# A decoder layer with dilated attention: the output matmuls of attention issued three steps behind their scores instead of two, with five buffers for the probabilities

## The chip, the cores and the metric

The kernel runs on one core of a Trainium2 chip. The time is device microseconds of one launch; the kernel before has a median of 2238.2 us over 3 runs (2236.06 to 2238.77).

## What is computed

One decoder layer over 4096 tokens of width 1024. The input is normalised per row and projected once; three groups of heads read the projection: 4 heads of a gated MLP over chunks of 128, 8 heads of causal attention in strided windows, 4 heads of attention over 256 memory tokens. Each is multiplied by a SiLU gate, concatenated, projected out and added to the input. The changed part is the strided attention:

```
for window, dil in ((128, 1), (512, 4), (2048, 16)):
    s = q . k / 8            # a block of 128 queries against its own and the previous block of keys
    s = where(0 <= rel <= window // dil, s, -inf)
    o_i, denominator_i = softmax(s) @ v
out = sum_i softmax(log denominators)_i * o_i
```

## The kernel before

**Passes.** Pass A (to about 650 us) normalises and transposes the input, and projects V and the first four heads' Q and K, which go to DRAM. Pass B projects the other four heads' Q and K and the gate of attention; pass C projects what the gated MLP and the memory heads need and computes both. The strided attention is a generator (`attn_all`), of which `merge` (line 59) takes some steps for each step of pass B and of pass C, at a higher priority. The output stage at the end (`fps`, line 937) is a run of matmuls of its own, from some 1870 us on.

**Attention of a head.** It has two stages. `attn_max` finds for each query the largest score of all three windows: 96 matmuls `pa` (line 467) go to PSUM tiles of which there are two, VectorE adds the mask and takes row maxima (`jk`, `mx`, line 474). The maxima are put into one layout by way of DRAM (`md`, line 482), of five transposes (`pm`, line 491) and of small DMAs into `cm` (lines 484 and 493), and VectorE takes their minimum with sign reversed (lines 495 and 497). `attn_main` then computes 48 steps, each of two query blocks. A step has its scores `s` by eight matmuls (lines 564 and 566; the second of a pair also subtracts the maximum, by a row of `q2` that a DMA fills from `cm`, line 512), adds the mask on VectorE (`e`, line 569), takes the exponential on ScalarE (line 571), and splits it into an F16 high half `ph` (ScalarE, line 520) and a low half `pl` (GpSimd, line 521). The output matmuls are three for each block of keys (lines 587, 589 and 591), with `ph`, `ph` and `pl` as weights; a step has up to twelve. Every four query blocks ScalarE copies the sum out (`ot`, line 596) and SyncE's queue writes it to `od`.

While the 48 steps of head h run, the maxima of head h+1 are computed between them (`mp_stage`, line 619), and near their end `q`, `k` and the rest of head h+1 are loaded (`load2`). `qn` and `kp`, which the maxima read, have one buffer; `vr`, the values, has three, of which a window uses two.

**The lag.** The output matmuls of a step are a closure that is put on a list `pend`; `drain(2)` issues all but the last two of the list, so a step's closure runs two steps after its scores, and `drain(0)` issues the rest at the end of a head. A step's closure reads its own `ph` and `pl` and those of the step before it (`prev`). `ph` and `pl` have four buffers each, which the memory heads share (line 799); `e` has four, the score PSUM tile two.

**Who sets the order.** The lines of the program give each instruction its priority; a scheduler then sets, when the kernel is built, the order on each engine by priorities and its own timeline, and places instructions that it takes to be ready. Engines run their queues in that order, one instruction after the other, and wait by semaphores.

Of the kernel before, what the change touches and what calls it, by code (L numbers as in the profile page):

```python
# [9 lines left out]
F16 = mybir.dt.float16  # L10
# [8 lines left out]
P = 128  # L19
# [52 lines left out]
def tile_hybrid_layer(ctx, tc, x, mem, norm_gain, w_in, gv_gain, wsT, gb, aqg, akg,  # L72
# [381 lines left out]
    at = at_cm.__enter__()  # L454
# [60 lines left out]
    G.memset(k2[64:65, :], 32768.0)  # L515

    def split_p(e, w, nm):
        ph = at.tile([P, 512], F16, name=f"ph{nm}", tag="ph", bufs=4)
        pl = at.tile([P, 512], F16, name=f"pl{nm}", tag="pl", bufs=4)
        S.copy(ph[:, :w], e[:, :w])  # L520
        G.tensor_sub(pl[:, :w], e[:, :w], ph[:, :w])  # L521
        return ph, pl

    def attn_main(h, q1, k1):
        pend = []

        def drain(k):
            while len(pend) > k:
                pend.pop(0)()

        for ci, d in list(enumerate(DILS))[::ORD]:
            nb = NT // d
            vts = []
            for i in range(2):
# [4 lines left out]
                else:  # L539
                    vt = at.tile([P, nb, d // 2, VW], F16, name=f"vr{h}_{ci}_{i}", tag="vr",  # L540
                                 bufs=3)
# [10 lines left out]
            for r in range(d):  # L552
                prev = None
                for b0 in range(0, nb, 2):
                    nm = f"{h}_{ci}_{r}_{b0}"
                    st = ps_tile("ps", [P, 2, 256], F32, f"s{nm}")
                    last = b0 + 2 >= nb
                    w = 384 if last else 512
                    for i in range(2):
                        b = b0 + i  # L560
                        k0 = r + b * P * d
                        n = 256 if b + 1 < nb else 128
                        kk = slice(k0, k0 + (P - 1) * d + 1, d)
                        TE.matmul(st[:, i, :n], k1[:, kk], packed(q1, d, r, b, n), start=True,  # L564
                                  stop=False)
                        TE.matmul(st[:, i, :n], k2[:, kk], packed(q2, d, r, b, n), start=False,  # L566
                                  stop=True)
                    e = at.tile([P, 512], F32, name=f"e{nm}", tag="e", bufs=4)
                    V.tensor_tensor(e[:, :w], st.rearrange("p a q -> p (a q)")[:, :w],  # L569
                                    masks[d][:, :w], ALU.add)  # L570
                    S.activation(e[:, :w], e[:, :w], AF.Exp, scale=asg[:, 2:3])  # L571
                    ph, pl = split_p(e, w, nm)

                    def pv(r=r, b0=b0, ph=ph, pl=pl, prev=prev, ci=ci, d=d, nb=nb, vblk=vblk, og=og):
                        for i in range(2):
                            b = b0 + i
                            slot = (r * nb + b) % 4
                            if slot == 0:
                                og[0] = ps_tile("po", [P, 4, 65], F32, f"o{h}_{ci}_{r}_{b}")
                            o = og[0]  # L580
                            terms = [(ph, pl, i * 256, b)]
                            if b:
                                terms.append((ph, pl, 128, b - 1) if i else
                                             (prev[0], prev[1], 384, b - 1))
                            for j, (hi, lo, c, vb) in enumerate(terms):
                                v = vblk(r, vb)
                                TE.matmul(o[:, slot, 0:65], hi[:, c:c + 128], v[:, 0:65],  # L587
                                          start=(j == 0), stop=False)
                                TE.matmul(o[:, slot, 0:64], hi[:, c:c + 128], v[:, 66:130],  # L589
                                          start=False, stop=False)  # L590
                                TE.matmul(o[:, slot, 0:65], lo[:, c:c + 128], v[:, 0:65],  # L591
                                          start=False, stop=(j == len(terms) - 1))
                            if slot == 3:
                                ot = at.tile([P, 4, 65], F32, name=f"ot{h}_{ci}_{r}_{b}", tag="ot",
                                             bufs=2)
                                S.copy(ot, o)  # L596
                                if d == 4:
                                    ov = o_d[ci].rearrange("(b m r j) h c -> r b m j h c", b=nb,
                                                           r=d, j=8)
                                    for i in range(4):  # L600
                                        Q.dma_start(ov[r, b - 3 + i, :, :, h, :], ot[:, i, :])
                                else:
                                    ov = o_d[ci].rearrange("(x p) h c -> p x h c", p=P)
                                    x1 = r * nb + b + 1
                                    Q.dma_start(ov[:, x1 - 4:x1, h, :], ot)

                    pend.append(pv)
                    drain(2)
                    prev = (ph, pl)
                    yield  # L610
        drain(0)
# [33 lines left out]
    def m_stage(h):  # L645
        cur[0] = h
        yield from attn_main(h, *mains[h])
# [119 lines left out]
    def mem_attn(n, qn):  # L767
        qd = pm.tile([P, 4, 2, HD], F16, name=f"qd{n}", tag="hl", bufs=2)
        q2t = q2ts[0]
        S.copy(qd, qn.unsqueeze(2).broadcast_to([P, 4, 2, HD]))  # L770
        V.tensor_sub(q2t[:, :, 0:64], qn, qd[:, :, 0, :])
        if n % 2 == 0:
            qms[0] = pm.tile([P, 2, 2, 4, P], F16, name=f"qm{n}", tag="stg", bufs=2)
        Q1m, Q2m = qms[0][:, n % 2, 0], qms[0][:, n % 2, 1]
        Q.dma_start_transpose(Q1m, qd.rearrange("p s a c -> p (s a c)"))
        m4 = pm.tile([P, 4], F32, name=f"m4{n}", tag="m4")
        for hp in range(2):
            pa = ps_tile("pa", [P, 2, 256], F32, f"mpa{n}_{hp}")
            for i in range(2):
                TE.matmul(pa[:, i, :], Q1m[:, 2 * hp + i, :], K1m[:, 2 * hp + i, :],  # L780
                          start=True, stop=True)
            V.tensor_reduce(m4[:, 2 * hp:2 * hp + 2], pa, AX.X, ALU.max)
        V.tensor_scalar(q2t[:, :, 64], m4, -(2.0 ** -15), msg[:, 3:4], ALU.mult, ALU.add)
        Q.dma_start_transpose(Q2m, q2t.rearrange("p s c -> p (s c)"))
        yield
        o = ps_tile("po", [P, 4, 65], F32, f"mo{n}")
        for hp in range(2):
            st = ps_tile("ps", [P, 2, 2, P], F32, f"ms{n}_{hp}")
            for i in range(2):
                h = 2 * hp + i  # L790
                for b in range(2):
                    kk = slice(b * P, (b + 1) * P)
                    TE.matmul(st[:, i, b, :], K1m[:, h, kk], Q1m[:, h, :], start=True,
                              stop=False)
                    TE.matmul(st[:, i, b, :], K2m[:, h, kk], Q2m[0:65, h, :], start=False,
                              stop=True)
            if not pools:
                e = at.tile([P, 512], F32, name=f"me{n}_{hp}", tag="e", bufs=4)
                ph = at.tile([P, 512], F16, name=f"mph{n}_{hp}", tag="ph", bufs=4)
                pl = at.tile([P, 512], F16, name=f"mpl{n}_{hp}", tag="pl", bufs=4)  # L800
            else:
                e = pools[0].tile([P, 512], F32, name=f"me{n}_{hp}", tag="fx", bufs=3)
                phl = pools[0].tile([P, 2, 512], F16, name=f"mp{n}_{hp}", tag="fx", bufs=3)
                ph, pl = phl[:, 0, :], phl[:, 1, :]
            S.activation(e, st.rearrange("p a b q -> p (a b q)"), AF.Exp, scale=msg[:, 2:3])
            S.copy(ph, e)
            G.tensor_sub(pl, e, ph)
            for i in range(2):
                h = 2 * hp + i
                for b in range(2):  # L810
                    c = (2 * i + b) * P
                    v = Vm[:, b, h, :]
                    TE.matmul(o[:, h, 0:65], ph[:, c:c + P], v[:, 0:65], start=(b == 0),
                              stop=False)
                    TE.matmul(o[:, h, 0:64], ph[:, c:c + P], v[:, 66:130], start=False,
                              stop=False)
                    TE.matmul(o[:, h, 0:65], pl[:, c:c + P], v[:, 0:65], start=False,
                              stop=(b == 1))
        rd = pm.tile([P, 4], F32, name=f"rd{n}", tag="rd")
        V.reciprocal(rd, o[:, :, 64])  # L820
        V.tensor_tensor(ym[n], o[:, :, 0:64], bcast(rd, HD), ALU.mult)
        yield
# [159 lines left out]
```

## Time and profile before

| | us |
|---|---|
| median of 3 runs | 2238.2 |
| profiled execution | 2232.59 |
| its span | 2230.9 |
| TensorE busy in it | 2018.8 |
| VectorE busy | 1568.5 |
| ScalarE busy | 1046.4 |
| GpSimd busy | 975.4 |

The profiled execution is one execution with the hardware profiler on; the span runs from its first to its last instruction. Engines are PE (TensorE), DVE (VectorE), ACT (ScalarE), POOL (GpSimd) and SP (SyncE, whose own queue is SPq and which issues the DMAs). A busy time is the union of the instructions' times; matmuls are pipelined, so a busy TensorE need not be one at its peak. Names are those of tiles in the program, with buffer numbers left out; `out<-in` says what an instruction writes and reads. `[6.87 <-DVE mx L474]` at the end of a row says that the engine was idle for 6.87 us just before it, and which instruction ended that.

### The profile page before, as it was taken

Reading aid. Unit: us, or ns where it says so; the run is one execution under the profiler, and the core shown is the slowest. Engines: PE = TensorE matmul, PEld = TensorE weight load, DVE = VectorE, ACT = ScalarE, POOL = GpSimd, SP = SyncE. Lnnn points to the kernel's source line nnn. Section 1 sums busy time; section 2 is a strip of 40 time slices with the busy share of each in tenths; the row PEclk is TensorE's granted clock in tenths of the full one; section 3 lists DMA queues with packets and bytes.
Section 4 is the critical chain, followed back from the end, with each engine's and each line's share of the span. In section 5 each row is a group of like instructions: output and inputs, shape, how many; then the busy total and the mean of one; then the engine's idle time right before and its main releaser. Section 6 shows DMA issues by size and latency. Waiting matters only on the chain. (4 is left out here: it accounts for less than half of the span.)

```text
span 2230.9 us, 44658 instructions
## 1 busy us (share of the span) xinstructions
PE 2018.8 (90%) x16481; PEld 1271.2 (57%) x16481; DVE 1568.5 (70%) x4297; ACT 1046.4 (47%) x1950; POOL 975.4 (44%) x696
## 2 busy tenths in 40 slices
PE   4888888978789899888999998998998999999998
PEld 3333333434346556455677676675775766666676
DVE  7776755477777867678688677776786667677662
ACT  5434433222236546456376465564675663222221
POOL 1455455465358657666365354453563550000000
PEclk8999998989899999999999999999999999999999
DMA  9989797775456674765545537446345347677762
GB/s 265 222 216 240 193 228 171 191 173 141 122 151 146 169 191 115 191 157 140 158 103 134 140 87 170 115 94 165 82 112 120 87 103 216 203 219 221 216 194 73
DMA packets 539675, 358.76 MB, mean 161 GB/s; under 512 B 365120, under 2 KB 474816, under 8 KB 537664
## 3 DMA queue, kind: packets, MB, share of 16 engines
q1 hardware_dynamic: 539456, 355.91, 62.8%
q8 instruction: 129, 2.11, 0.4%
q14 instruction: 90, 0.74, 0.1%
HBM read 198.52 MB, written 113.84 MB: 140 GB/s over the span
## 5 line engine op out<-in xcount | busy, mean ns | idle before, releaser
L521 POOL TENSOR_TENSOR pl<-e,ph 128x512 f16<-128x512 f32 (+1 forms) x384 | 414.8, 1095 | 305.7 <-ACT ph L520 228.9
L222 PE MATMUL pc<-wC,xTc 128*128 128x512 f16 (+1 forms) x2304 | 477.1, 351 | 6.0 <-DVE r_wO L160 5.2
L474 DVE CUSTOM_DVE_ANT_0 jk<-pa,mask 128x256 bf16<-128x256 f32 (+1 forms) x768 | 302.7, 394 | 60.9 <-PE pa L467 42.1
L222 PE MATMUL fps<-wO,fyT 128*128 128x256 f16 (+1 forms) x2304 | 341.2, 309 | 0.0
L571 ACT ACTIVATE e<-e,gas 128x512 f32<-128x512 f32 (+1 forms) x384 | 253.0, 673 | 178.7 <-DVE e L569 176.1
L222 PEld LDWEIGHTS <-xTc 128*128 128x128 f16 x2304 | 223.8, 101 | 158.6 <-issue 15.3
L222 PEld LDWEIGHTS <-xTa 128*128 128x128 f16 x1608 | 164.4, 103 | 258.4 <-issue 89.6
L569 DVE TENSOR_TENSOR e<-s,mask 128x512 f32<-128x512 f32 (+1 forms) x384 | 234.1, 626 | 69.8 <-PE s L566 50.4
L222 PEld LDWEIGHTS <-fyT 128*128 128x128 f16 x2304 | 224.5, 98 | 101.9 <-issue 1.6
L222 PEld LDWEIGHTS <-xTb 128*128 128x128 f16 x1536 | 152.0, 101 | 178.5 <-issue 28.1
L222 PE MATMUL pv<-wV,xTa 128*128 128x512 f16 (+1 forms) x840 | 194.3, 394 | 49.4 <-DVE vt L276 34.4
L520 ACT CAST ph<-e 128x512 f16<-128x512 f32 (+1 forms) x384 | 211.5, 567 | 28.8 <-PE o L591 19.0
L222 PE MATMUL pqb<-wQ,xTb 128*128 128x512 f16 x768 | 195.7, 398 | 13.1 <-DMA xTb<-xTd 8.9
L291 POOL COPY stpA<-stgA 128x1024 f16<-128x1024 f16 x32 | 153.4, 4820 | 102.0 <-DMA stgA<-hl 55.9
L291 POOL COPY stpB<-stgB 128x1024 f16<-128x1024 f16 x32 | 153.5, 4798 | 97.2 <-DMA stgB<-hl 84.1
L564 PE MATMUL s<-q,k 128*128 128x256 f16 (+1 forms) x768 | 180.3, 266 | 15.1 <-DMA q<-qkpd 5.4
L222 PE MATMUL pag<-wAG,xTb 128*128 128x512 f16 x768 | 186.3, 386 | 3.8 <-DVE sg L699 3.5
L222 PE MATMUL pq<-wQ,xTa 128*128 128x512 f16 x768 | 176.9, 388 | 12.2 <-ACT rw_q L248 8.1
L467 PE MATMUL pa<-kp,qn 128*128 128x256 f16 (+1 forms) x768 | 138.7, 270 | 52.0 <-DVE mx L474 38.0
L566 PE MATMUL s<-q,k 65*128 65x256 f16 (+1 forms) x768 | 172.1, 266 | 3.7 <-DMA q<-cm 3.7
L587 PE MATMUL o<-vr,ph 128*128 128x65 f16 x1368 | 169.5, 194 | 2.9 <-ACT ot L596 1.8
L591 PE MATMUL o<-vr,pl 128*128 128x65 f16 x1368 | 159.6, 193 | 11.1 <-POOL pl L521 11.0
(274 smaller groups left out, 3511.5 us busy)
## 6 DMA issues: line engine op xcount, KB each, us to landing
vr<-vd SPq DMA_DIRECT2D x48, 520.0 KB
fo<-od SPq DMA_DIRECT2D x96, 260.0 KB
od<-ot SPq DMA_DIRECT2D x128, 130.0 KB
x_a<-in_x_dram SPq DMA_DIRECT2D x32, 512.0 KB
xTd<-xTa SPq DMA_DIRECT2D x32, 512.0 KB
xTb<-xTd SPq DMA_DIRECT2D x32, 512.0 KB
xTc<-xTd SPq DMA_DIRECT2D x32, 512.0 KB
fx<-in_x_dram SPq DMA_DIRECT2D x32, 512.0 KB
```

Source lines behind the costliest of these rows:

```text
L222: TE.matmul(ps[:, :n], xt[:, a, k, :], w[:, b, k, c:c + n], start=(k == 0 and a == 0 and b == 0), stop=(k == KT - 1 and a == 1))
L291: G.tensor_copy(stp[:, :, half].rearrange("p s (r j) -> p s j r", r=R16), stg[:, :, half].rearrange("p s (j r) -> p s j r", r=R16))
L467: TE.matmul(pa[:, i, 256 - w:256], qn[:, q0:q0 + (P - 1) * d + 1:d], packed(kp, d, r, max(b - 1, 0), w), start=True, stop=True)
L474: V.tensor_tensor_reduce(jk[:, :w], pa[:, i, 256 - w:256], masks[d][:, 256 - w:256], 1.0, -3e38, ALU.add, ALU.max, mx[:, mc:mc + 1])
L520: S.copy(ph[:, :w], e[:, :w])
L521: G.tensor_sub(pl[:, :w], e[:, :w], ph[:, :w])
L564: TE.matmul(st[:, i, :n], k1[:, kk], packed(q1, d, r, b, n), start=True, stop=False)
L566: TE.matmul(st[:, i, :n], k2[:, kk], packed(q2, d, r, b, n), start=False, stop=True)
L569: V.tensor_tensor(e[:, :w], st.rearrange("p a q -> p (a q)")[:, :w], masks[d][:, :w], ALU.add)
L571: S.activation(e[:, :w], e[:, :w], AF.Exp, scale=asg[:, 2:3])
L587: TE.matmul(o[:, slot, 0:65], hi[:, c:c + 128], v[:, 0:65], start=(j == 0), stop=False)
L591: TE.matmul(o[:, slot, 0:65], lo[:, c:c + 128], v[:, 0:65], start=False, stop=(j == len(terms) - 1))
```

## The change

The list `pend` keeps three closures instead of two before one is issued, and `ph` and `pl` have five buffers instead of four, in `split_p` and where the memory heads take tiles of the same tag. Nothing else is edited.

```
     def split_p(e, w, nm):
-        ph = at.tile([P, 512], F16, name=f"ph{nm}", tag="ph", bufs=4)
-        pl = at.tile([P, 512], F16, name=f"pl{nm}", tag="pl", bufs=4)
+        ph = at.tile([P, 512], F16, name=f"ph{nm}", tag="ph", bufs=5)
+        pl = at.tile([P, 512], F16, name=f"pl{nm}", tag="pl", bufs=5)
...
                     pend.append(pv)
-                    drain(2)
+                    drain(3)
...
-                ph = at.tile([P, 512], F16, name=f"mph{n}_{hp}", tag="ph", bufs=4)
-                pl = at.tile([P, 512], F16, name=f"mpl{n}_{hp}", tag="pl", bufs=4)
+                ph = at.tile([P, 512], F16, name=f"mph{n}_{hp}", tag="ph", bufs=5)
+                pl = at.tile([P, 512], F16, name=f"mpl{n}_{hp}", tag="pl", bufs=5)
```

Since the scheduler sets the order, it comes out anew on all engines from the first steps of attention on. Three places follow. Heads are numbered from 0, and a name carries its head first: `jk3_0_2` is a row maximum of head 3.

VectorE's queue at the change to head 2, in the kernel before (`cm2` holds the maxima of head 2, `jk3`, `mx3` and `pa3` belong to the maxima of head 3):

```order
L269 TENSOR_TENSOR rw_q1_28_9928<-rw_q1_28_9928,gaq_591 128x256
L495 TENSOR_TENSOR cm2_9347<-cm2_9347 32x128
L497 TENSOR_TENSOR cm2_9347<-cm2_9347 32x8x16
L288 TENSOR_TENSOR hl1_28_9942<-rw_q1_28_9928,hl1_28_9942 128x8x64
L474 ISA jk3_0_0_9629,mx3_9625<-pa3_0_0_9626,mask1_739 128x128
```

The same place in the changed kernel:

```order
L474 ISA jk3_0_0_9619,mx3_9615<-pa3_0_0_9616,mask1_739 128x128
...
L474 ISA jk3_0_1_9621,mx3_9615<-pa3_0_0_9616,mask1_739 128x256
...
L474 ISA jk3_0_2_9697,mx3_9615<-pa3_0_1_9694,mask1_739 128x256
...
L474 ISA jk3_0_3_9699,mx3_9615<-pa3_0_1_9694,mask1_739 128x256
...
L495 TENSOR_TENSOR cm2_9334<-cm2_9334 32x128
```

Four row maxima of head 3, which read its first two `pa` tiles, have moved ahead of line 495.

TensorE's queue at the same place, weight loads left out, in the kernel before:

```order
L467 MATMUL pa3_0_0_9626<-kp_3_9621,qn_3_9620 128x256
...
L467 MATMUL pa3_0_1_9706<-kp_3_9621,qn_3_9620 128x256
...
L467 MATMUL pa3_0_2_9735<-kp_3_9621,qn_3_9620 128x256
...
L467 MATMUL pa3_0_3_9766<-kp_3_9621,qn_3_9620 128x256
...
L566 MATMUL s2_2_1_0_9510<-q2_3666,k2_3667 128x256
```

And in the changed kernel (the projection `pag` stands 14 times, the output matmuls between the first and the last that are shown are 24):

```order
L467 MATMUL pa3_0_1_9694<-kp_3_9611,qn_3_9610 128x256
...
L222 MATMUL pag26_10026<-wAG_3719,xTb26_9385 128x512
...
L587 MATMUL o1_0_0_28_9448<-vr1_0_1_8667,ph1_0_0_28_9313 128x65
...
L591 MATMUL o1_0_0_28_9448<-vr1_0_1_8667,pl1_0_0_30_9361 128x65
...
L467 MATMUL pa3_0_2_9725<-kp_3_9611,qn_3_9610 128x256
```

The last output matmuls of head 1 and a projection have come between the second and the third `pa` of head 3, where the `pa` stood next to each other.

VectorE's queue at the change to head 5, in the kernel before, from the fourth row maximum of head 6 on:

```order
L474 ISA jk6_0_4_17321,mx6_17220<-pa6_0_2_17318,mask1_739 128x256
...
L474 ISA jk6_0_6_17352,mx6_17220<-pa6_0_3_17349,mask1_739 128x256
...
L474 ISA jk6_0_8_17433,mx6_17220<-pa6_0_4_17430,mask1_739 128x256
...
L495 TENSOR_TENSOR cm5_16871<-cm5_16871 32x128
L474 ISA jk6_0_9_17435,mx6_17220<-pa6_0_4_17430,mask1_739 128x256
```

And in the changed kernel:

```order
L474 ISA jk6_0_2_17243,mx6_17210<-pa6_0_1_17240,mask1_739 128x256
...
L474 ISA jk6_0_3_17245,mx6_17210<-pa6_0_1_17240,mask1_739 128x256
...
L495 TENSOR_TENSOR cm5_16858<-cm5_16858 32x128
L497 TENSOR_TENSOR cm5_16858<-cm5_16858 32x8x16
L474 ISA jk6_0_4_17311,mx6_17210<-pa6_0_2_17308,mask1_739 128x256
```

Here line 495 has moved the other way: it follows four row maxima of head 6 where it followed nine.

## Rows read from the trace of the kernel before

**Rows 1.** The page: span; busy us, share of the span, instructions of two engines

```profile
span 2230.9 us, 44658 instructions
PE 2018.8 (90%) x16481; PEld 1271.2 (57%) x16481; DVE 1568.5 (70%) x4297; ACT 1046.4 (47%) x1950; POOL 975.4 (44%) x696
```

**Rows 2.** Windows by stage: busy us and count of each engine, granted clock, DMA

```profile
660.00:1825.00 1165.00, 1080.70 (x10906) 745.35 (x10905) 864.47 (x2672) 701.43 (x1395) 648.05 (x509) 0.97 0.54 131
...
1825.00:1925.00 100.00, 96.32 (x806) 66.04 (x804) 73.93 (x191) 35.62 (x45) 10.18 (x9) 0.97 0.75 211
1925.00:2231.00 306.00, 299.70 (x2325) 210.49 (x2322) 190.80 (x461) 75.17 (x74) 0.00 (x0) 1.00 0.61 185
```

**Rows 3.** Waits of PE over the span: us in total, times, longest

```profile
PE pa L467 <- DVE mx L474: 38.0, 27, 6.9
...
PE o L591 <- POOL pl L521: 11.0, 20, 1.1
...
PE pa L467 <- DMA qn<-qnd: 8.2, 4, 3.4
...
PE s L564 <- DMA q<-qkpd: 5.4, 2, 2.8
...
PE s L566 <- DMA q<-cm: 3.7, 3, 2.8
...
PE s L564 <- DMA k<-knd: 3.2, 1, 3.2
...
PE o L587 <- ACT ph L520: 1.0, 2, 0.5
```

**Rows 4.** Timeline of PE, change to head 2: start, us, instruction, idle before

```profile
939.65 0.44 PE L564 MATMUL s<-q,k 128*128 128x256 f16 x2 [2.85 <-DMA q<-qkpd]
...
951.74 0.58 PE L467 MATMUL pa<-kp,qn 128*128 128x256 f16 x2 [6.87 <-DVE mx L474]
...
952.78 0.58 PE L467 MATMUL pa<-kp,qn 128*128 128x256 f16 x2 [0.46 <-DVE mx L474]
...
953.85 0.37 PE L566 MATMUL s<-q,k 65*128 65x256 f16 x1 [0.49 <-DMA q<-cm]
```

**Rows 5.** Timeline of DVE, change to head 2

```profile
945.31 3.97 DVE L495 TENSOR_TENSOR cm<-cm 32x128 f16<-32x128 f16 x1 [6.83 <-DMA cm<-rw]
...
950.47 0.27 DVE L474 CUSTOM_DVE_ANT_0 jk<-pa,mask 128x128 bf16<-128x128 f32 x1
```

**Rows 6.** Window behind it

```profile
950.00:960.00 10.00, 7.09 (x47) 5.32 (x47) 8.66 (x35) 4.42 (x10) 2.78 (x3) 0.51 0.58 152
```

**Rows 7.** Instructions of `ph`: count, ns min/median/max, first and last start

```profile
L587 PE MATMUL o<-vr,ph x1368: 191/193/262, 656.5 to 1823.4; 128*128 128x65 f16 x196
...
L520 ACT CAST ph<-e x384: 493/602/635, 655.9 to 1815.5; 128x512 f16<-128x512 f32 x128, 128x384 f16<-128x384 f32 x64
L521 POOL TENSOR_TENSOR pl<-e,ph x384: 907/1156/1611, 656.5 to 1816.1; 128x512 f16<-128x512 f32 x128, 128x384 f16<-128x384 f32 x64
```

**Rows 8.** Timeline of PE: first and last output matmul of the last 24

```profile
1822.75 0.19 PE L587 MATMUL o<-vr,ph 128*128 128x65 f16 x1
...
1823.45 0.19 PE L591 MATMUL o<-vr,pl 128*128 128x65 f16 x1
```

**Rows 9.** Timeline of PE: 19 projection matmuls in a row

```profile
1449.84 4.26 PE L222 MATMUL pc<-wC,xTc 128*128 128x512 f16 x19
```

**Rows 10.** Timeline, change to head 5

```profile
1396.68 0.21 DVE L495 TENSOR_TENSOR cm<-cm 32x128 f16<-32x128 f16 x1 [4.46 <-DMA cm<-rw]
...
1402.15 0.31 PE L566 MATMUL s<-q,k 65*128 65x256 f16 x1 [2.79 <-DMA q<-cm]
```

**Rows 11.** Timeline, change to head 4

```profile
1249.65 0.21 DVE L495 TENSOR_TENSOR cm<-cm 32x128 f16<-32x128 f16 x1 [8.92 <-DMA cm<-rw]
1251.61 0.38 PE L467 MATMUL pa<-kp,qn 128*128 128x256 f16 x2 [0.72 <-DVE mx L474]
```

**Rows 12.** Waits of SyncE's queue

```profile
SPq L605 <- ACT ot L596: 130.8, 56, 9.0
...
SPq L543 <- PE o L591: 19.6, 9, 4.4
```

**Rows 13.** Waits of ACT

```profile
ACT ph L520 <- PE o L591: 19.0, 18, 2.9
```

**Rows 14.** Instructions of line 495: ns min/median/max

```profile
L495 DVE TENSOR_TENSOR cm<-cm x8: 204/212/3970, 644.2 to 1686.1; 32x128 f16<-32x128 f16 x8
```

**Rows 15.** Timeline of POOL, change to head 2

```profile
945.12 4.71 POOL L291 COPY stpB<-stgB 128x1024 f16<-128x1024 f16 x1 [7.82 <-DMA stgB<-hl]
```

## The prediction

> **What bounds the kernel now.** I read the page's busy shares first, then the windows by stage, the waits of TensorE, and last the timeline around the moments where the kernel passes from one attention head to the next. TensorE is the engine that bounds: it is busy 2018.8 us of a span of 2230.9, the next one, VectorE, 1568.5 [rows 1]. The windows split this. While attention runs (660 to 1825 us) TensorE is busy 1080.7 of 1165 us; in the 100 us behind it 96.3, and in the last 306 us 299.7 [rows 2]. So what is left to win in the changed stage is at most the 84.3 us that are not busy there, and whatever the tail does, it is full already: attention that ends a little sooner or later is worth its own TensorE time and nothing more.
>
> The waits of TensorE say what the idle time is made of [rows 3]. Waiting for the low halves of the probabilities (`pl`), the wait that a longer lag attacks by its nature, costs 11.0 us in 20 waits, the longest 1.1 us; the high halves (`ph`) cost 1.0 us. More is waited for the maximum of the next head (`pa` behind `mx`, 38.0 us over the whole run) and for what is loaded at a change of head: `qn` 8.2, `q` from `qkpd` 5.4, `q` from `cm` 3.7, `k` 3.2 us.
>
> The change to head 2 (heads are numbered from 0; the maxima of head 2 are done, its scores and the maxima of head 3 begin) shows how these belong together [rows 4, 5]. TensorE sits idle 2.85 us before the first score, then 6.87 us before the maximum matmuls of the next head, with 0.46 and 0.49 us behind. VectorE in that time waits 6.83 us for a DMA of `cm`, at line 495; the row maxima (L474) that free the two PSUM buffers of `pa` stand behind that instruction in its queue and start at 950.47. After it the granted clock is 0.51 of full speed over 950 to 960 us [rows 6], that is mostly the 1.2 GHz level, with 7.09 us of TensorE work in it.
>
> **The change part by part.** No arithmetic is added or removed: the same 1368 matmuls of each of the three kinds, 384 casts, 384 subtractions [rows 7]. Moved is each step's group of output matmuls, one step later, with what follows from it: the eviction `ot`, the `od` writes on SyncE's queue, the release of `ph`, `pl` and of `vr`. From 656.5 to 1823.4 us there are 384 steps, so a step lasts 3.04 us on average.
>
> *Waits for `pl` and `ph` on TensorE: 11.0 + 1.0 us [rows 3].* The ends are 0 and -12.0 us. One step more is worth 3.04 us, and the longest of these waits is 1.1, so a strict shift would take all of them. But the order of the instructions is made by a scheduler that already puts other work in between: counted in the order of before, 175 of the 384 groups of output matmuls come with three younger steps' scores already issued, 137 with two; in the order of the change 205 come with three and 81 with four. About a third of the groups move, so I take a third: -4.
>
> *The change to head 2.* The order shows that in the changed kernel four row maxima stand ahead of line 495, which free both `pa` buffers, and that TensorE has 14 matmuls of 128x512 and 24 output matmuls between the second and the third `pa`. The ends: nothing of the 7.33 us (6.87 + 0.46) and of the 2.85 + 0.49 us is saved; or all 10.67, and with it the slow clock, under which 7.09 us of work take as long as 3.5 at the other level, so 3.5 us more. The wait for `cm` itself stays, and TensorE's new cover there is less than what VectorE waits: 24 output matmuls pass in 0.73 us (first at 1822.75, last at 1823.45, one step of 0.03 behind it) [rows 8], and 14 wide ones pass in 3.1, at the 4.26 us of a row with 19 [rows 9]. I take -6 of the waits and -2 of the clock: -8.
>
> *First scores of the other heads.* Counted between the last transpose of the maxima (L491) and the first matmul of L566, the order has 585 matmuls in seven changes of head before and 837 now, because more output matmuls (24 or 36 more in five of the seven) and projections with them stand there. These cover the wait for `q` from `cm`, 3.7 us in 3 [rows 3], of which 2.79 falls at the change to head 5 [rows 10]. Ends 0 and -3.7; I take -2.
>
> *The change to head 5, on the other side.* Line 495 now stands behind four row maxima of the next head instead of nine. In the kernel before VectorE waited 4.46 us there for `cm` [rows 10] with no long wait of TensorE behind it; at the change to head 4 it waited 8.92 [rows 11]. What TensorE would wait now is not in the trace. Ends: 0, when the `pa` that have their buffers last as long as the wait, and 6.87 + 3.5 = 10.4 us, when what happened at head 2 repeats itself here. I take +4, nearer to the row of this place, which is 4.46 less a little cover.
>
> *The last steps of the last head.* Three groups are left behind the last scores instead of two. One is 12 matmuls, half of the 24 in 0.73 us, so +0.4; the tail behind is 96% busy [rows 2] and hides the writes.
>
> *SyncE's queue.* The reload of a `vr` buffer waits for the last output matmul that reads it; it waited 19.6 us in 9 cases, and `od` writes waited 130.8 us for `ot` [rows 12]. Both come up to one step, 3.04 us, later, and everything queued behind on SyncE with them. TensorE has no wait for `vr` in its list, so this is hidden by the third `vr` buffer: 0. With the cover gone, one such reload per configuration would cost up to 3.04 us each.
>
> *Five buffers instead of four.* ScalarE's cast waited 19.0 us for an output matmul to release `ph` [rows 13]. The lag takes up the buffer that is added, so this stays as it is; ScalarE is busy 1046.4 us of the span [rows 1] and its wait is not on the path: 0. The `e` tiles (four) and the score PSUM tiles (two) are as they were, and a score step can't run further ahead than these let it.
>
> One rule of the Trainium skill bears on the change to head 2. There the small operation of line 495 took 3.97 us, while its other executions have a median of 0.212 [rows 5, 14], and GpSimd ran the 4.71 us copy of `stpB` from 945.12 on [rows 15]. The page "SBUF — State Buffer", section "Who interferes with whom", says that a VectorE instruction with two SBUF inputs contends with a GpSimd instruction that reads SBUF, and that who comes first holds the port; the trace agrees. By that rule 3.76 us of the wait there are luck of the hour and could come back at any place where the copy and line 495 meet; the term would then be -8 + 3.76 and the whole sum -5.8.
>
> **Sum.** -4 - 8 - 2 + 4 + 0.4 = -9.6 us. The profiled execution took 2232.6 us (span 2230.9 and 1.7 around it); the median of the timed runs is 2238.2, 5.6 higher. 2238.2 - 9.6 = 2228.6; I write 2229. With every term at its good end the sum is -12 - 14.2 - 3.7 + 0.4 = -29.5 us, with every term at its bad end 10.4 + 0.4 = +10.8; that all meet one end is unlikely, and the middle between -29.5 and -9.6 is 2218.6. So the likeliest case's own range is 2218 to 2234.
>
> **The rivals.**
>
> *No change.* The scheduler has put the output matmuls where their inputs are ready in both orders; the shift only shuffles. For it: waits for `pl` are 11.0 us of a span of 2230.9, half a per cent, and the median distance between a step's scores and its first use of `pl`, counted by columns in the order, hardly moves. Against it: the concrete new order at the change to head 2. What is won there would then be paid back at head 5 and at loads that come with less work beside them: 2238, within 4.5 us.
>
> *Slower.* Line 495 blocks VectorE with the row maxima behind it, not at one place but two, the changes to heads 5 and 6, where line 495 stands 14 and 26 rows behind line 480, which ends the maxima, instead of 41 and 29. It decides once VectorE's wait for `cm` there is longer than the work that TensorE has up to its third `pa`. Price: two times 6.87 + 0.46 of wait and 3.5 of clock, 21.7 us, with the gains of -14 kept only in half: 2238.2 + 21.7 - 7 = 2253. With one place it is 2242. For it: VectorE waited 6.83 and 8.92 us at this line at two of the changes. Against it: at head 4, behind the 8.92 us, TensorE waited only 0.72 for `mx` [rows 11].
>
> **How the numbers follow.** The forecast, faster by about 9 us, gets 0.5; no change 0.26; slower 0.24. Two kernels that differ by less than 0.2%, 4.5 us, can't be told apart here. The forecast's case lies almost wholly below 2233.7 and the others hardly give to it: faster 0.50, same 0.27, slower 0.23. The range begins at 2214, about three quarters of the way from the sum to its good end, and goes up to 2246, which holds no change, the slower case with one place, and the way to the one with two up to half.
>
> **What would show it.** Right: in the changed kernel's trace the wait of `pa` for `mx` at the change to head 2 is under 2 us and the clock behind it near 1; waits of TensorE for `pl` sum to some 7 us instead of 11. Wrong: a wait of 4 us or more of `pa` for `mx` at the change to head 5 or 6, line 495 of VectorE idle ahead of it; or waits for `vr` or `qn` on TensorE that grow by more than 5 us together. Wrong in its root would be a TensorE that waits as long as before in sum, at other places.

## The result and the profile after

The changed kernel is slower, by 0.6%. Its median is 2248.5 us (2240.4 to 2257.8, 12 runs) against 2236.1 us (2229.6 to 2242.9, 12 runs) of the kernel before on the same chip; the ratio estimated from all these runs is 1.0061, 95% interval 1.0045 to 1.0078 (the two medians alone give 1.0055). The forecast was 2229 us, faster by 9.6; the time lies above the top of its range (2246) as well.

The profiled execution took 2253.3 us, its span is 2251.6, 20.7 more than before; that is more than the 12.4 between the medians, because this one execution lies above its median and the profiled one of before (2232.6) below its own. The page after, in the columns of [rows 1]:

```profile
span 2251.6 us, 44556 instructions
PE 2018.4 (90%) x16481; PEld 1272.7 (57%) x16481; DVE 1581.9 (70%) x4297; ACT 1047.4 (47%) x1950; POOL 973.0 (43%) x696
```

TensorE does what it did: 2018.4 us and 16481 matmuls, 2018.8 and as many before. The whole difference is idle time of TensorE. The windows by stage, cut at the first output matmul of line 591 (661.1 us, 657.5 before), at the last one (1836.9, before 1823.5), and 94 us behind it:

```profile
661.00:1837.00 1176.00, 1082.82 (x10899) 746.09 (x10899) 881.07 (x2676) 704.70 (x1399) 648.12 (x511) 0.97 0.54 130
1837.00:1931.00 94.00, 84.18 (x736) 59.49 (x733) 66.80 (x173) 30.61 (x42) 11.08 (x9) 0.96 0.71 193
1931.00:2251.00 320.00, 314.93 (x2432) 220.28 (x2430) 200.46 (x481) 80.16 (x79) 0.00 (x0) 1.00 0.62 187
```

Against [rows 2]: attention has 93.2 us without TensorE work where it had 84.3, and the stretch behind it is 90% busy where it was 96%. From these three times 20.7 us divide into 3.6 ahead of the first output matmul, 9.8 from the first to the last (1166.0 to 1175.8), and 7.3 behind (407.4 to 414.7). The first part is not the change's: up to 664 us of the kernel before (668 of the changed one) all engines have the same instructions in the same order in both traces, so 3.6 us is what two executions of one order differ by there. The granted clock of attention is 0.97 both times, so the clock isn't the cause.

TensorE's waits, in the columns of [rows 3]:

```profile
PE pa L467 <- DVE mx L474: 34.5, 31, 3.4
PE s L564 <- DVE e L569: 20.5, 29, 3.7
PE pa L467 <- DMA qn<-qnd: 16.8, 6, 6.4
...
PE o L591 <- POOL pl L521: 8.5, 13, 1.8
...
PE s L564 <- DMA q<-qkpd: 5.6, 1, 5.6
PE ms L795 <- DMA qm<-q2t: 5.2, 4, 2.6
...
PE s L566 <- DMA q<-cm: 1.0, 2, 0.6
```

and the row of before that the prediction didn't read, since it was small:

```profile
PE s L564 <- DVE e L569: 4.7, 12, 0.7
```

The reader sees two things. What the change was to shorten is shorter: `pl` 11.0 to 8.5, `q` from `cm` 3.7 to 1.0, `mx` 38.0 to 34.5; and `k`, 3.2 us before, has gone from the list. What grew stands elsewhere: the scores of a step wait for VectorE's mask `e` to free a score tile, 4.7 to 20.5 us, and the maxima wait for `qn`, 8.2 to 16.8. All of TensorE's waits in the list together went from 204.9 to 224.8 us, +19.9 of the 20.7: 6.9 of it ahead of the first output matmul, where the order is the same, 7.2 in attention (84.1 to 91.3) and 5.7 behind it (4.0 to 9.7). So in attention most of what `e` and `qn` cost more is made up for by waits that became shorter, and the net loss is smaller than either row suggests.

What such a wait for `e` looks like. TensorE in the changed kernel, then VectorE just ahead of it (start, us, instruction, idle before):

```profile
1725.31 0.37 PE L564 MATMUL s<-q,k 128*128 128x256 f16 x1 [3.68 <-DVE e L569]
```

```profile
1716.56 1.01 DVE L569 TENSOR_TENSOR e<-s,mask 128x384 f32<-128x384 f32 x2
1718.14 0.42 DVE L849 TENSOR_TENSOR rw_c<-rw_c,r_c 128x256 f32<-128x256 f32 x1 [0.57 <-POOL r_c L260]
...
1720.64 2.29 DVE L145 TENSOR_REDUCE m_wO<-st_wO 128x8 f32<-128x2048 f32 x1 [1.74 <-DMA st_wO<-in_w_out_dram]
1722.85 0.68 DVE L782 TENSOR_REDUCE m<-mpa 128x2 f32<-128x512 f32 x1
...
1723.77 0.69 DVE L782 TENSOR_REDUCE m<-mpa 128x2 f32<-128x512 f32 x1
...
1724.70 1.02 DVE L569 TENSOR_TENSOR e<-s,mask 128x384 f32<-128x384 f32 x2
```

Between two pairs of `e` VectorE does work of the other streams: a scaling of pass C, a reduction over the output weights (it waits 1.74 us for a DMA and then takes 2.29), maxima of the memory heads. TensorE's next scores need a score tile that this `e` frees, and what stands behind them in its queue waits with them. No output matmul and no probability buffer stands in these rows.

The long waits for `qn` are at changes of head, where `qn` has one buffer. In the changed kernel, then the same matmuls at the second of these places in the kernel before (at the first it waited 0.15 us):

```profile
791.57 0.90 PE L467 MATMUL pa<-kp,qn 128*128 128x128 f16 x4 [6.42 <-DMA qn<-qnd]
...
1396.50 0.91 PE L467 MATMUL pa<-kp,qn 128*128 128x128 f16 x4 [4.94 <-DMA qn<-qnd]
```

```profile
1379.95 0.59 PE L467 MATMUL pa<-kp,qn 128*128 128x128 f16 x4 [3.44 <-DMA qn<-qnd]
```

The change to head 2, on which the prediction rested most, came out as forecast. VectorE there (compare [rows 5]):

```profile
949.57 0.42 DVE L474 CUSTOM_DVE_ANT_0 jk<-pa,mask 128x256 bf16<-128x256 f32 x1
...
953.48 1.63 DVE L495 TENSOR_TENSOR cm<-cm 32x128 f16<-32x128 f16 x1 [3.15 <-DMA cm<-rw]
```

and the window of [rows 6] behind it:

```profile
950.00:960.00 10.00, 9.43 (x68) 4.73 (x65) 6.57 (x18) 3.90 (x7) 4.77 (x1) 1.00 0.58 164
```

Four row maxima run ahead of line 495, the 6.87 us of TensorE are gone, and the clock is 1.00 where it was 0.51. In 30 us around line 495 TensorE's waits fell from 11.9 to 2.2. The lower clock came a little later instead (0.72 from 970 to 980 us), and over attention it is 0.97 as before. Line 495 itself again meets GpSimd's copy of `stpB`, and takes 1.63 us where the median of its executions is 0.212:

```profile
950.90 4.77 POOL L291 COPY stpB<-stgB 128x1024 f16<-128x1024 f16 x1 [3.52 <-DMA stgB<-hl]
```

That agrees once more with the Trainium skill ("SBUF — State Buffer", section "Who interferes with whom"), by which a VectorE instruction with two SBUF inputs contends with a GpSimd instruction that reads SBUF. Over all traces of this case: line 495 takes 0.20 to 0.22 us wherever GpSimd is idle beside it, and 0.39 to 4.03 where it meets a copy of `stpB`; beside GpSimd's short `r_c` and `r_q` alone it stays at 0.20 to 0.21. Its price here is 1.4 us on VectorE, and TensorE had work.

### The profile page after: what moved, and what is told of

The parts are those of the page before. It is cut to its first block, busy times and chain, and to the rows that moved or that the text cites. A ratio compares the mean times of both kernels' runs of the same rounds, so it can differ in the third digit from the quotient of the medians.

```text
span 2251.6 us, 44556 instructions
## 1 busy us (share of the span) xinstructions
PE 2018.4 (90%) x16481; PEld 1272.7 (57%) x16481; DVE 1581.9 (70%) x4297; ACT 1047.4 (47%) x1950; POOL 973.0 (43%) x696
## 5 line engine op out<-in xcount | busy, mean ns | idle before, releaser
L222 PE MATMUL pv<-wV,xTa 128*128 128x512 f16 (+1 forms) x840 | 188.9, 386 | 51.2 <-DVE vt L276 37.8
L564 PE MATMUL s<-q,k 128*128 128x256 f16 (+1 forms) x768 | 179.3, 265 | 27.7 <-DVE e L569 20.5
L467 PE MATMUL pa<-kp,qn 128*128 128x256 f16 (+1 forms) x768 | 137.7, 269 | 56.2 <-DVE mx L474 34.5
```

The lines of the kernel that those rows point to most:

```text
L222: TE.matmul(ps[:, :n], xt[:, a, k, :], w[:, b, k, c:c + n], start=(k == 0 and a == 0 and b == 0), stop=(k == KT - 1 and a == 1))
L467: TE.matmul(pa[:, i, 256 - w:256], qn[:, q0:q0 + (P - 1) * d + 1:d], packed(kp, d, r, max(b - 1, 0), w), start=True, stop=True)
```

## The experiments

Three readings of the loss were put to the test. **A**: the lag itself costs, since scores come ahead of output matmuls that used to stand between them, and TensorE then waits for VectorE to free a score tile. **C**: the fifth buffer costs, since with it the steps bunch in the same way; **A2** joins the two (a longer lag or a fifth `ph` lets score steps run ahead). **B**: the edit makes the scheduler deal out all engines' work anew, and the new order is a worse one, whatever the edit was for. **D** is the placing of tiles in memory, which an added buffer moves. All runs stand beside runs of the kernel before on their own chip (median of these 2247 to 2249 us; 2236 on the chip of the result), 5 rounds each. The last two columns are TensorE's waits in sum and its wait of scores for `e`, from one profiled execution of each. The row of before is a short execution on the chip of the result; pl5_only, which has the same order of instructions on every engine, shows how far such sums differ without a cause in the kernel: 220.3 against 204.9. The wait for `e` is steadier: 5.6 against 4.7.

| kernel | lag | buffers | ratio to before, 95% interval | waits us | for `e` |
|---|---|---|---|---|---|
| before | 2 | 4 | 1 | 204.9 | 4.7 |
| after (the result) | 3 | 5 | 1.0061 [1.0045, 1.0078] | 224.8 | 20.5 |
| bufs5_lag2 | 2 | 5 | 1.0074 [1.0057, 1.0091] | 229.0 | 19.3 |
| lag1 | 1 | 4 | 1.0006 [0.9995, 1.0017] | 216.7 | 8.7 |
| ph5_only | 2 | `ph` 5, `pl` 4 | 1.0134 [1.0115, 1.0153] | 247.0 | 13.7 |
| pl5_only | 2 | `ph` 4, `pl` 5 | 0.9999 [0.9981, 1.0016] | 220.3 | 5.6 |
| own_mem_lag2 | 2 | 4 + 1 | 1.0025 [1.0010, 1.0040] | 227.5 | 7.6 |
| own_mem_lag3 | 3 | 4 + 1 | 1.0106 [1.0087, 1.0126] | 233.7 | 14.0 |
| lag1_bufs3 | 1 | 3 | 1.0199 [1.0170, 1.0228] | 241.2 | 18.9 |
| lag1_bufs5 | 1 | 5 | 1.0057 [1.0036, 1.0078] | 229.9 | 20.4 |
| shuffle_c_lag2 | 2 | 4 | 1.0001 [0.9986, 1.0017] | 220.0 | 8.2 |
| shuffle_c_lag3 | 3 | 5 | 1.0039 [1.0025, 1.0052] | 224.6 | 11.4 |
| shuffle_r_lag2 | 2 | 4 | 1.0173 [1.0138, 1.0209] | 250.4 | 16.1 |
| shuffle_r_lag3 | 3 | 5 | 1.0097 [1.0075, 1.0120] | 228.8 | 14.8 |
| shuffle_u_lag2 | 2 | 4 | 1.0040 [1.0024, 1.0056] | 225.1 | 13.3 |
| shuffle_u_lag3 | 3 | 5 | 1.0043 [1.0026, 1.0059] | 221.3 | 17.0 |

### Each part of the change alone

Buffers without the lag (the changed kernel with `drain(2)`), and the lag the other way without buffers (the kernel before with `drain(1)`):

```
# bufs5_lag2                          # lag1
-                    drain(3)         -                    drain(2)
+                    drain(2)         +                    drain(1)
```

> Only the five buffers, the lag stays two. Theory A (the lag itself costs: scores are issued before output matmuls that used to stand between them, and TensorE then waits for VectorE to free one of the two score PSUM tiles): as before within 5 us, PE's wait of s for DVE e near its 4.7 us, not near the 20.5 of the changed kernel. Theory B (any edit makes the scheduler deal out a new order, and a new order is worth up to 15 us either way, whatever the edit): a time that may differ from before by 5 to 15 us, with waits at new places. Theory C (the buffers cost, not the lag): slower by 8 to 14 us.

> Lag one with four buffers. Theory A: PE's wait of s for DVE e falls under 4 us, its waits of o for pl and ph grow well over 12 us; the time is then a balance, between 2236 and 2256. Theory B: no order in the waits by lag; a time anywhere from 2225 to 2255.

Five buffers alone cost 0.74%, no less than the whole change, and the wait for `e` is 19.3 us where A had forecast some 4.7; a shorter lag costs nothing that shows, and its wait for `e` is 8.7, not under 4. So the loss does not need the longer lag (A), and this pair alone spoke for the buffers (C).

### One ring at a time

The kernel before with only one of the two tags at five, in `split_p` and in the memory heads:

```
# ph5_only: tag="ph", bufs=4  ->  bufs=5
# pl5_only: tag="pl", bufs=4  ->  bufs=5
```

> Lag two, five buffers for the high halves alone, four for the low halves. Theory C, as the runs so far leave it (with four high-half buffers ScalarE's cast waits for output matmuls to release one, and that spaces the steps; with five it doesn't, ScalarE's wait of ph for o falls from 19 to about 5 us, the steps bunch, and TensorE waits for VectorE to free a score tile): slower than before by 8 us or more, wait of s for DVE e 11 us or more, wait of ph for o under 8 us. Theory B (the luck of the order): any time from 10 faster to 15 slower.

> Lag two, five buffers for the low halves alone. The order on all engines is that of the kernel before; only the places of tiles in SBUF and the waits of a low half for its buffer differ. Theory C and theory B both: as before within 4 us. Theory D (the new places of tiles in SBUF cost): slower by 8 us or more.

The two halves differ: a fifth `ph` costs 1.34%, a fifth `pl` nothing. Five `pl` buffers leave the order of the instructions on every engine as it was, all along the trace, and only place the tiles elsewhere, and the time is the same within 0.2%: that takes D away for `pl`, and it is the control of the whole study, for it says that the same order gives the same time. It gives the same stops too: the longest wait for `mx`, 6.9 us before, is there again, and line 495 again takes 3.98 us beside the copy of `stpB`, so that meeting belongs to the order. The waits of pl5_only:

```profile
PE pa L467 <- DVE mx L474: 42.3, 32, 7.0
...
PE s L564 <- DVE e L569: 5.6, 13, 0.8
```

In the profile of ph5_only ScalarE's cast, which waited 19.0 us for output matmuls [rows 13], waits 2.1, and TensorE pays for other things:

```profile
ACT ph L520 <- PE o L591: 2.1, 3, 1.5
```

```profile
PE pa L467 <- DVE mx L474: 47.1, 34, 4.7
...
PE s L564 <- DVE e L569: 13.7, 12, 2.7
```

By C this would be the fifth buffer's doing.

### The ring without the memory heads

The attention keeps four buffers for itself, and the memory heads take one `ph` and one `pl` of their own; with lag 2 and with lag 3:

```
-                ph = at.tile([P, 512], F16, name=f"mph{n}_{hp}", tag="ph", bufs=4)
-                pl = at.tile([P, 512], F16, name=f"mpl{n}_{hp}", tag="pl", bufs=4)
+                ph = at.tile([P, 512], F16, name=f"mph{n}_{hp}", tag="mph", bufs=1)
+                pl = at.tile([P, 512], F16, name=f"mpl{n}_{hp}", tag="mpl", bufs=1)
```

> Lag two, four buffers for the strided attention alone; the memory heads get one of their own for ph and for pl, so five in sum. Theory C: the spacing by ScalarE's wait stays in the strided attention (ph for o some 15 us), within 5 us of before, s for DVE e under 9 us. If the loss comes with the memory heads' share of the ring: slower by 8 us.

> As the last, with the lag three: the lag of the changed kernel without a fifth buffer for the strided attention. Theory C: within 5 us of before; theory A (the lag costs): slower by 8 to 14 us, s for DVE e 15 us or more.

Lag 3 with four buffers in attention is slower than lag 2 with four, by 0.8%. Taken alone this spoke for A again, against the pair above. Two readings, each held up by one pair and refuted by the next, suggest a third cause that is in all of them.

### Lag 1 with three and with five buffers

```
# lag1_bufs3: drain(1), both tags bufs=3 at all four places
# lag1_bufs5: drain(1), both tags bufs=5 at all four places
```

> Lag one and three buffers for both halves. Theory A2 (the score steps may run further ahead with a longer lag or with a fifth high-half buffer; then they bunch, TensorE waits for VectorE to free a score tile, and 9 to 30 us are lost in sum; with lag two or less and four buffers they don't): s for DVE e under 10 us, time at most 0.3% over before. Theory B (each edit draws a new order; the order before happens to be a good one, and new ones are 0 to 1.3% slower without regard to lag or buffers): any time from as before to 1.3% slower, s for DVE e not tied to the number of buffers.

> Lag one with five buffers. Theory A2: s for DVE e over 10 us and 0.3 to 1.3% slower than before, as with lag two and five. Theory B: no such tie; it may come out as lag one with four did (as before) or anywhere up to 1.3%.

Fewer buffers are no cure: three cost 1.99%, and there ScalarE waits long for output matmuls to release `ph`:

```profile
ACT ph L520 <- PE o L591: 98.6, 68, 5.1
```

So C in its simple form (the fewer run ahead, the better) fell, and A2, which had forecast at most 0.3%. Lag 1 with five costs 0.57%, as A2 forecast, and there ScalarE's wait is 0.7 us. With five buffers the lag makes no difference that shows: lags 1, 2 and 3 give 1.0057, 1.0074 and 1.0061.

### Edits that mean nothing

`merge` takes some steps of attention for each step of pass B or C, and the ratio is a number in the code. Three kernels of before have that number changed by half a per cent, with lag 2 and four buffers kept; three others have the same edit in the changed kernel. No lag, no buffer and no operation differs within either set:

```
# shuffle_c_lag2, shuffle_c_lag3
-    merge(tc, pass_c(), side, 5 * 52 / (0.85 * 160), 1)
+    merge(tc, pass_c(), side, 5 * 52 / (0.855 * 160), 1)
# shuffle_r_lag2, shuffle_r_lag3
-    merge(tc, pass_b(), side, 190/62.0, 2)
+    merge(tc, pass_b(), side, 189/62.0, 2)
# shuffle_u_lag2, shuffle_u_lag3
+    merge(tc, pass_b(), side, 191/62.0, 2)
```

> Lag two and four buffers as before, but the ratio at which attention steps are dealt to pass C is half a per cent smaller, a change without a meaning of its own that gives a new order. Theory A: as before within 5 us, s for DVE e under 8 us. Theory B: differs from before by 5 to 15 us.

> The changed kernel with the same half per cent in the ratio of pass C. Theory A: 8 to 14 us slower than the kernel with lag two and this ratio, s for DVE e 15 us or more. Theory B: the difference to it may have either sign.

> Lag two, four buffers, half a per cent less in the ratio at which attention steps are dealt to pass B. Theory A2: within 0.3% of before, s for DVE e under 10 us. Theory B: may be slower by up to 1.3%.

> The changed kernel (lag three, five buffers) with half a per cent less in the ratio of pass B. Theory A2: 0.3 to 1.3% slower than before, s for DVE e over 10 us. Theory B: may be as fast as before.

> Lag 2, four buffers, as before; only the ratio by which the row projections of pass B are mixed with the attention goes from 190/62 to 191/62. Theory 'new order': the scheduler deals the work out anew, so 0 to +2 % against before (1.000 to 1.020), not faster by more than 0.2 %; the wait of the scores for VectorE's e is 9 us or less if the ratio is under 1.003 and 11 us or more if it is over 1.004. Theory 'the lag is what costs': 1.000 +- 0.002.

> The changed kernel (lag 3, five buffers) with the same ratio of 191/62. Theory 'new order': 1.000 to 1.020, in no fixed relation to its partner of lag 2; the two pairs so far gave +0.4 and -0.8 % for lag 3 over lag 2. Theory 'the lag is what costs': slower than its partner by 0.4 to 0.8 %, as in the case itself.

These show that neither part of the change is needed for such a loss. With lag 2 and four buffers, a ratio of 189 in place of 190 costs 1.73%, nearly three times what the change costs. Its waits have the look of the changed kernel's; first shuffle_r_lag2, then shuffle_r_lag3:

```profile
PE pa L467 <- DVE mx L474: 34.9, 31, 4.3
PE pa L467 <- DMA qn<-qnd: 23.3, 5, 6.6
PE s L564 <- DVE e L569: 16.1, 18, 4.4
PE ms L795 <- DMA qm<-q2t: 15.9, 5, 11.7
```

```profile
PE pa L467 <- DVE mx L474: 32.1, 28, 3.6
PE pa L467 <- DMA qn<-qnd: 17.5, 6, 4.6
PE s L564 <- DVE e L569: 14.8, 18, 2.2
```

The scores wait 16.1 us for `e` and `qn` takes 23.3, without a fifth buffer and without a third step of lag; so these waits need neither. The other two such edits cost 0.01 and 0.40%. And with that ratio lag 3 is the faster one.

There are now four pairs that differ by the change alone, in four dealings of the order. Lag 3 with five buffers over lag 2 with four, as the quotient of the ratios, and the differences of the profiled executions, one of each kernel (output matmuls of line 591; the tail is what follows the last):

| ratio of pass B, of pass C | lag 3 over lag 2 | first to last output matmul us | tail us |
|---|---|---|---|
| 190, 0.85 (the case) | +0.61% | +9.8 | +7.3 |
| 190, 0.855 | +0.38% | -0.7 | +6.9 |
| 189, 0.85 | -0.75% | -26.2 | +8.6 |
| 191, 0.85 | +0.03% | -9.4 | +11.4 |

The mean of the four is +0.07%, and they reach from -0.75 to +0.61. By itself the change neither wins nor loses anything that four dealings can show: by their spread, the 95% interval of the mean is -0.9 to +1.0%. Only the tail moves one way; there 19 to 52 more matmuls are left behind the last output matmul (3143 to 3162, 3132 to 3184, 3079 to 3123, 3143 to 3189), so part of it is work that was shifted and not added. And single profiles carry it: in pl5_only the tail is 5.4 us longer than in the kernel before, with the same order.

### A third score tile

To learn whether the wait for `e` is what costs, or only marks an order that costs, before and after were given three score tiles; the edit takes the room for the third in PSUM from the tag `po` (output sums, and the transposes `pm` and `fpt`), which gets one tile instead of two:

```
-        return pp.tile(shape, dt, tag="po" if tag == "tr" else tag, name=name)
+        t = "po" if tag == "tr" else tag
+        return pp.tile(shape, dt, tag=t, name=name, bufs={"ps": 3, "po": 1}.get(t, 2))
```

> Before with three PSUM tiles for scores instead of two and one for outputs instead of two (the eight banks allow no more). It is a new order too. Theory 'the wait of the scores for e is the cost of a slow order': this wait falls below 3 us and the time is within 0.5 % of before unless the waits of the output matmuls for the single output tile's eviction grow by 10 us or more. Theory 'the wait is only a mark of a slow order': the wait falls and the time is 0.5 to 2 % over before all the same.

> The changed kernel with three PSUM tiles for scores and one for outputs. Theory 'the wait of the scores for e is the cost': against 20.5 us in the changed kernel it falls below 5 us, and the ratio to before falls from 1.006 to 1.000 or below, unless waits for the single output tile take its place (10 us or more in the output matmuls). Theory 'only a mark': the ratio stays between 1.004 and 1.020.

Neither came true: the ratios are 1.071 [1.068, 1.074] and 1.060 [1.057, 1.062]. The waits of scores3_lag2 (its line numbers are one higher):

```profile
PE fpt L748 <- DVE fhl L743: 39.1, 21, 3.4
...
PE s L565 <- DVE e L570: 29.5, 38, 3.2
...
PE o L588 <- ACT ot L597: 16.2, 16, 2.5
```

The single tile of `po` costs 16.2 us in attention and 39.1 in the transposes `fpt` (1.8 and 2.0 us in the kernel before); and the wait for `e` did not fall, it rose to 29.5 us (21.3 with lag 3). So the question stays open. The Trainium skill ("Perfetto Trace Analysis", section "Optimization Strategy") says that bubbles which repeat can mean too little SBUF or PSUM for the next tile; the runs here agree for the output tile and do not bear it out for the buffers of `ph` (ph5_only) or, as far as this run tells, for the score tile. What follows is only that one more score tile, paid for with an output tile, doesn't end that wait, and that with one tile of `po` the kernel loses far more than in any other run here; how much of that is the tile and how much the new order, these two runs can't part.

## Why the prediction was wrong

**Its named terms.** Most came near, as far as they can be read. Waits for `pl`: -2.5 us and for `ph` -0.5 (1.0 to 0.5) against a term of -4. The change to head 2: the wait of 6.87 us is gone, and `pa` waits 5.3 us less for `mx` over attention (22.2 to 16.9), near the -6 of the term of -8; the sign that was to show it right (the wait there under 2 us) is there. Its -2 for the clock does not show, since the lower clock came later. Also what the prediction called luck of the hour, line 495 beside the copy, is not luck: pl5_only, with the same order, repeats it. First scores: `q` from `cm` -2.7 against -2. The loss at the change to head 5 that was priced at +4 did not come: TensorE's waits in 55 us around line 495 there sum to 10.8 before and 10.9 after. `qn` is 4.94 us late at 1396.50, but it was 3.44 late before, and the waits for `q` that stood there before are gone. Line 495 waits less for `cm` in sum:

```profile
DVE cm L495 <- DMA cm<-rw: 8.6, 4, 3.6
```

It was 22.4 us before. So the rival "slower" had the sign, and its mechanism, VectorE held at line 495 with row maxima behind it, did not happen.

**The step that failed** is the bound of the sum: "Moved is each step's group of output matmuls, one step later, with what follows from it". The sum took four places where the order was seen to change and left the rest of the 2231 us at what the trace of before showed. But the front part itself says that the order comes out anew on all engines, and then each of the waits that were small before is a number drawn anew too, the ones in no list above all. What the runs show in its place: a new order by itself, with nothing else changed, cost between nothing that shows and 1.73%, and that was priced nowhere. The wait of scores for `e`, +15.8 us, stood at 4.7 in the trace and in no term; `qn`, +8.6, stood only in what would show the prediction wrong, and it did: "waits for `vr` or `qn` on TensorE that grow by more than 5 us together". Also the sentence that it would be wrong in its root with "a TensorE that waits as long as before in sum, at other places" is what happened, with 7.2 us more in attention and 19.9 over the profile, 6.9 of them where the order is the same.

**A second error was in one term.** "The lag takes up the buffer that is added, so this stays as it is": ScalarE's wait for output matmuls fell instead:

```profile
ACT ph L520 <- PE o L591: 3.7, 4, 1.3
```

19.0 to 3.7 us [rows 13]. In the order only about a third of the groups moved, which would leave the fifth buffer partly free; that was not shown. It gave nothing, as was forecast. A ScalarE that runs ahead is not needed for such a loss either, since shuffle_r_lag2, which is slower yet, still has 22.1 us of that wait:

```profile
ACT ph L520 <- PE o L591: 22.1, 21, 4.1
```

**The tail** was taken as full, from one trace of before. In the changed kernel the 94 us behind attention are busy for 84.2; but in pl5_only, with the order of before, they are busy for 86.5, against 90.3 before. So most of this reading was one execution's, and not the order's.

**What "no change" had.** This rival said that the shift only shuffles, and priced the shuffle at nothing, "within 4.5 us". The first half is what the pairs show. The price is what was missing: over the 14 new orders that were run with two score tiles (the result's own among them, pl5_only not, whose order is the old one), the ratio is 1.000 to 1.020, and no estimate is below 1. Only three of these are edits without a meaning in the kernel before (1.000, 1.004 and 1.017). The last pair, whose forecast was this range, came out inside it. The order of before is a good draw, and an edit that changes the order gives it up.

**What stays open.** Which placements make one order worse than another was not settled. The wait of scores for `e` sorts them: up to 8.7 us where the ratio is at most 1.0025, 11.4 or more where it is at least 1.0039. It is only part of the loss (11.4 of the 45.5 us of waits that shuffle_r_lag2 has more than before, of which the control pl5_only has 15.4 without a new order), and the run that should have taken it away did not. Four pairs don't tell a cost or a gain of the change of up to 0.9% from none. Nor is a small price of the fifth `ph` ruled out: all seven kernels with five `ph` are slower by 0.39% or more and wait 11.4 us or more for `e`, 0.72% in the mean, while the five new orders with four `ph` and lag 1 or 2 (lag1, own_mem_lag2 and the three edits without a meaning) lie between 0.01 and 1.73%, 0.49% in the mean. Lag 3 with four shared buffers, and a fifth `e` tile, were not tried.

## What to carry to other kernels

Where a scheduler sets the order, an edit of any line is two edits: what it says, and a new order everywhere. Price the second by an edit that means nothing (a ratio changed by half a per cent) before the first is believed: here it was worth 0.0 to 1.7%, the change itself +0.07% in the mean over four orders with pairs from -0.75 to +0.61. A forecast for such a kernel starts from that distribution, and where the present order is the best that has been seen, the distribution lies on the slow side. Here most terms read off single places came near, and the time still went the other way.

Compare pairs in several orders before naming a cause: two pairs here (five buffers with lag 2, and lag 3 with four buffers in attention), each sound by itself, pointed at two different causes, and the other pairs bore out neither. And keep one control whose order is the old one: it tells how much of a difference between two profiles is no cause at all, here 15.4 us of waits.
